# A hybrid decoder layer on one core: the first 512 tokens' q projection, by token tile or by block of input features

## The chip, the core and the metric

The kernel runs on one core of a Trainium2 chip. The metric is the device time of one execution in microseconds (us), lower is better. Before the change the runs shown gave a median of 1939.51 us (three runs, 1933.7 to 1939.64).

The engines are named as in the profile: PE (TensorE; PEld is its weight load), ACT (ScalarE), DVE (VectorE), POOL (GpSimd), SP (SyncE, which here only issues DMAs). SPq and ACTq are the sequencers of SP and ACT, which issue DMAs in order.

## The reference

x has 2048 tokens of 1024 features, all in float32. The layer is

```python
h = rms_norm(x, attn_norm_g)
z = h @ w_in                     # 512 q, 128 k, 128 v, 3 x 512 conv columns
q, k = rms_norm(q), rms_norm(k)  # per head of 64
y_attn = swa_sink_attention(q, k, v, sinks)      # window 128
y_conv = gate_b * short_conv(gate_c * xc, conv_w)
x = x + concat(rms_norm(y_attn), rms_norm(y_conv)) @ w_out
hm = rms_norm(x, mlp_norm_g)
x = x + square(relu(hm @ w_up)) @ w_down
```

The part that the change touches is `z = h @ w_in` for the first 512 tokens and the first 768 columns (q, k, v).

## The kernel before, in words

**Products.** Each float32 operand is split into a high part (rounded to PE's float32r format, by ACT) and a low part (the rest, by DVE). A product is three matmuls: high by high, high by low, low by high. In the projections to z's rows the stationary operand is a 128x128 block of h (features by tokens) and the moving one 256 or 512 columns of the weights.

**Chunks.** The mixers (attention, convolution, output projection) run over four chunks of 512 tokens, each of four token tiles of 128. While the attention of chunk c goes on, `besides` (line 941) does beside it chunk c's convolution and half of its output projection, then chunk c+1's norm, transposes and q/k/v projection; `fill` with the counts of `FILL` decides how the two are interleaved, and the priorities in `PRIO` steer the scheduler. After the mixers comes the MLP, in blocks of 512 (lines 1096 to 1545), which the change leaves as it is.

**The first chunk's start** (lines 436 to 541) has its order written out by hand for all engines (`manual_schedule`). x0 are four token tiles [128 tokens, 1024 features], loaded on SP: tile 0 in two halves, then the first 256 columns of w_in in two halves of input features, then tiles 1 to 3, then the next 256 columns. PE first turns `SPIN[0]` = 5 idle matmuls, then the transposes of tile 0 (`moved(0, 0)`, line 468), then `SPIN[1]` = 3 idle ones. ACT makes h's high part with the gain of attn_norm (line 474), DVE the low part (line 476), in pieces of 128 by 128; ACT and DVE split the weights (lines 458, 459). The norm's 1/rms is not in h: it is applied where z is copied out of PSUM (`put_z`, line 493). `product0` (line 488) then does one token tile after the other for columns 0 to 255. Columns 256 to 511 and 512 to 767 (k and v) follow in `project_qkv(0, ...)` (lines 557 to 578), four token tiles each, through the general helper `mm3` (lines 266 to 268). Line 1058 then transposes the 1/rms values, and the convolution's first product (pc_c) starts.

**Buffers.** Raw weights go through two `raw` buffers of [128, 2048]; split weights through four `w` buffers of that size. Two further sets matter for the change: `wop` (four buffers of [128, 2, 512], which later hold the convolution's outputs yt and the MLP's weights) and `at` (five of that size, which hold the attention's outputs). Split weights are stored to DRAM once (`keep`, line 228) and fetched by the later chunks, so that the split is done once; for q a later chunk fetches, for each half of the input features, two parts of two column pieces (line 585). x0's tiles are at the same time the rows that the residual sum is added to (line 892).

**Queues.** SP issues nearly all loads and stores in program order: the gains (lines 1061 to 1082) behind the first loads, and among them the k/v weights (line 239).

PSUM has eight banks: three `mm`, four `at`, one `tr`.

Of the kernel before, what the change touches and what calls it, by code (L numbers as in the profile page):

```python
# [7 lines left out]
F32 = mybir.dt.float32  # L8
# [8 lines left out]
P = 128  # L17
# [62 lines left out]
SPIN = (5, 3)  # L80
# [22 lines left out]
def hymba_layer(  # L103
# [99 lines left out]
    n_pieces = [0]  # L203
# [232 lines left out]
    x0 = [row("x1", f"x0_{t}", NT) for t in range(NT)]  # L436
    z0 = [zrow(f"z0_{t}") for t in range(NT)]
    raw0, raw1 = (raw_part(f"raw_qkv{pc}") for pc in range(2))
    hl0, hl1 = (high_low(0, f"w_qkv{pc}") for pc in range(2))
# [9 lines left out]
    def load_x0(t, cut=1):  # L449
        for i in range(cut):  # L450
            r = slice(i * D // cut, (i + 1) * D // cut)
            nc.sync.dma_start(x0[t][:, r], xf[t * P : (t + 1) * P, r])

    load_w0 = lambda i: nc.sync.dma_start(*cols256(wi, 0, pieces=2)(raw0)[i])

    def split0(i, raw, hl):
        r = slice(i * 512, (i + 1) * 512)
        nc.scalar.copy(hl[0][:, r], raw[:, r])
        nc.vector.tensor_tensor(hl[1][:, r], raw[:, r], hl[0][:, r].bitcast(F32), op=ALU.subtract)

    def moved(t, part):

        for i in range(2):
            kk = i * (KD // 2)
            if not part:
                pts[t, i] = bank("at", f"pt_a0_{t}_{i}")
                for j in range(4):
                    nc.tensor.transpose(pts[t, i][:, j * P : (j + 1) * P], x0[t][:, (kk + j) * P : (kk + j + 1) * P], ident)
            else:
                p3 = pts.pop((t, i)).rearrange("p (k t) -> p k t", k=4)  # L470
                dh, dl = (d[:, kk : kk + 4, t * P : (t + 1) * P] for d in h)
                for k in range(KD // 2):
                    g = g_in[kk + k]
                    nc.scalar.activation(dh[:, k], p3[:, k], AF.Copy, scale=g)
                for k in range(KD // 2):
                    nc.vector.scalar_tensor_tensor(
                        dl[:, k], p3[:, k], g_in[kk + k], dh[:, k].bitcast(F32), op0=ALU.mult, op1=ALU.subtract
                    )

    w0 = [w.rearrange("p (k c) -> p k c", k=KD) for w in hl0]  # L480

    def product0(t, i, ks=range(KD)):

        if (i, ks[0]) == (0, 0):
            pzs[t] = bank("mm", f"pz0_0_{t}")[:, :256]
        a, b = ((0, 0), (1, 0), (0, 1))[i]
        for k in ks:
            nc.tensor.matmul(
                pzs[t], h[a][:, k, t * P : (t + 1) * P], w0[b][:, k, :], start=i + k == 0, stop=i + k == KD + 1
            )  # L490

    def put_z(t):
        nc.scalar.activation(z0[t][:, :256], pzs[t], AF.Copy, scale=rs0[:, t : t + 1])

    pts, pzs = {}, {}

    with tc.manual_schedule(engines={ET.PE, ET.Activation, ET.DVE, ET.Pool, ET.SP}):
        nc.scalar.dma_start(g_rows, attn_norm_g[0].rearrange("(k p) -> k p", p=P))
        nc.scalar.activation(warm, mhalf[:, :1], AF.Square)
        load_x0(0, cut=2)  # L500
        load_w0(0)
        load_w0(1)
        for t in range(1, NT):
            load_x0(t)
        nc.sync.dma_start(*cols256(wi, 256)(raw1)[0])
# [11 lines left out]
        moved(0, 0)  # L517
        moved(0, 1)
        spin(SPIN[1])
        for i in range(4):  # L520
            split0(i, raw0, hl0)
            product0(0, 0, range(2 * i, 2 * i + 2))
            if i == 1:
                moved(1, 0)
        product0(0, 1)
        product0(0, 2)
        for t in range(1, NT):
            moved(t, 1)
            for i in range(4 if t + 1 == NT else 0):
                split0(i, raw1, hl1)  # L530
            norm_stats(x0[t - 1], f"a0_{t - 1}", rs0[:, t - 1 : t])
            if t > 1:
                put_z(t - 2)
            if t + 1 < NT:
                moved(t + 1, 0)
            for i in range(3):
                product0(t, i)
        norm_stats(x0[NT - 1], f"a0_{NT - 1}", rs0[:, NT - 1 : NT])
        put_z(NT - 2)
        put_z(NT - 1)  # L540
        rs0_in = nc.gpsimd.tensor_tensor(rs0_2, rs0, rs0, op=ALU.mult).ins


    with tc.tile_pool(name="mix_small", bufs=1) as mix_small, tc.tile_pool(name="mix", bufs=1) as mix:
# [10 lines left out]
        def project_qkv(c, h, z):  # L555

            z += z0 if not c else [zrow(f"z{c}_{t}") for t in range(NT)]
            if not c:
                keep(hl0, "qkv0")
            if not c:  # L560
                keep(hl1, "qkv1")
                for pc in range(1, 3):
                    hl = weights(cols256(wi, pc * 256), c, f"qkv{pc}") if pc > 1 else hl1
                    w4 = [w.rearrange("p (k c) -> p k c", k=KD) for w in hl]
                    for t in range(NT):
                        ps = bank("mm", f"pz{c}_{pc}_{t}")[:, :256]
                        hk = lambda s, k, t=t: h[s][:, k, t * P : (t + 1) * P]
                        for k in range(KD):
                            mm3(ps, lambda s, k=k: hk(s, k), lambda s, k=k: w4[s][:, k, :], k == 0, k == KD - 1)
                            if k % 2 and k < KD - 1:  # L570
                                yield
                        z_in.append(
                            nc.scalar.activation(
                                z[t][:, pc * 256 : (pc + 1) * 256], ps, AF.Copy, scale=rs0[:, t : t + 1]
                            ).ins
                        )
                        yield
                return

            both = []  # L580
            for half in range(2):
                hl = high_low(c, f"w_q{half}_{c}")
                for i in range(2):
                    for pc in range(2):
                        nc.sync.dma_start(
                            hl[i].bitcast(F32).rearrange("p (k c) -> p k c", k=KD // 2)[:, :, pc * 256 : (pc + 1) * 256],
                            parts_dram[f"qkv{pc}"][i].rearrange("p (k c) -> p k c", k=KD)[
                                :, half * (KD // 2) : (half + 1) * (KD // 2)
                            ],
                        )  # L590
                both.append([w.rearrange("p (k c) -> p k c", k=KD // 2) for w in hl])
# [982 lines left out]
```

## Time and profile before

| | before |
|---|---|
| median of the runs shown | 1939.51 us (1933.7 to 1939.64) |
| the profiled execution | 1936.33 us |
| its span, first to last instruction | 1934.6 us |
| PE busy | 1916.7 us |
| DVE, ACT, POOL busy | 1206.7, 837.7, 273.3 us |
| matmuls recorded | 9025 |
| data moved by DMA | 412.25 MB, mean 213 GB/s |

A line of the timeline gives start and duration in us, the engine, the line of the kernel, the operation, what it writes and reads by the program's names with the shapes, and how many were merged (x8); in brackets the idle time of the engine ahead of it and what ended that. A line of a group has the summed busy time and the mean in ns behind the bar, then the idle time of the engine just before, with the releasers. A line of the windows view has the stretch, its length, then busy time and count for PE, PEld, DVE, ACT and POOL, the clock that was granted to PE (1.00 is full), the share of the DMA engines' time and the GB/s moved. A line of the waits has who waited, for whom, the us in total, the number of times and the longest.

### The profile page before, as it was taken

How to read it: one execution, taken by the hardware profiler on the slowest of the kernel's cores; microseconds unless marked ns; L12 is line 12 of the kernel's file. 1: busy time of each engine (PE TensorE's matmuls, PEld its weight loads, DVE VectorE, ACT ScalarE, POOL GpSimd, SP SyncE). 2: the span in 40 equal slices, each digit the busy share in tenths (PEclk: the TensorE clock that was granted, in tenths of full speed). 3: DMA queues.
4: the chain of work that ended last, by engine and by line, in shares of the span. 5: the costliest groups of instructions: out<-in, count | busy, mean ns of one | idle time of the engine just before them, and what ended most of it. 6: DMA issues, size and time to landing. Idle time of an engine off the chain costs nothing.

```text
span 1934.6 us, 24806 instructions
## 1 busy us (share of the span) xinstructions
PE 1916.7 (99%) x9025; PEld 1596.0 (82%) x9025; DVE 1206.7 (62%) x1872; ACT 837.7 (43%) x1593; POOL 273.3 (14%) x473
## 2 busy tenths in 40 slices
PE   9999999999999999999999999999999999999999
PEld 9888888888888788888877888888888888888887
DVE  4885667447556768899878766666534334448541
ACT  6563445345344437445465554554422333232220
POOL 1112203312221112222201111101000000100000
PEclk9999999999999999999999999999999999999999
DMA  9774855464474787877665544437964457776631
GB/s 324 274 261 150 288 223 188 169 255 155 163 276 170 241 299 277 250 216 249 227 222 191 180 162 143 164 123 295 376 218 151 143 163 229 262 229 219 211 135 55
DMA packets 240634, 412.25 MB, mean 213 GB/s; under 512 B 51704, under 2 KB 147968, under 8 KB 228736
## 3 DMA queue, kind: packets, MB, share of 16 engines
q1 hardware_dynamic: 211824, 335.15, 51.3%
q0 software_dynamic: 15424, 51.40, 6.8%
q10 hardware_dynamic: 13264, 24.13, 3.3%
q8 instruction: 71, 1.16, 0.2%
q14 instruction: 51, 0.42, 0.1%
HBM read 284.78 MB, written 125.83 MB: 212 GB/s over the span
## 4 chain that ended last, share of the span: by engine, by line
PE 84%; issue 5%; DVE 4%; DMA 4%; ACT 2%; POOL 1%; SPq 1%; ACTq 0%; POOLq 0%; DVEq 0%
PE d L1534 31%; PE u L1427 23%; PE pout L266 2%; PE pout L268 2%; PE pout L267 2%; PE pz L266 2%; PE pz L267 2%; PE pz L268 2%; PE pc_c L266 2%; PE px_c L266 2%; PE px_c L267 2%; PE px_c L268 2%; PE pc_c L268 2%; PE pc_c L267 2%; PE psc_b L665 1%
## 5 line engine op out<-in xcount | busy, mean ns | idle before, releaser
L1427 PE MATMUL u<-op_x,wop 128*128 128x512 f32 x2688 | 612.5, 390 | 3.0 <-DVE wop L417 1.3
L1534 PE MATMUL d<-op_w,op_f 128*128 128x512 f32 x2688 | 609.4, 389 | 0.0
L1427 PEld LDWEIGHTS u<-op_x,wop 128*128 128x128 f32 x2688 | 503.7, 188 | 111.4 <-DVE wop L417 4.0
L1534 PEld LDWEIGHTS d<-op_w,op_f 128*128 128x128 f32 x2688 | 504.7, 188 | 104.6
L398 DVE TENSOR_TENSOR op_f<-op_f 128x1024 fp32r<-128x1024 f32 x112 | 136.9, 1225 | 237.8 <-ACT op_f L397 237.4
L397 ACT CAST op_f<-op_f 128x1024 fp32r<-128x1024 f32 x112 | 118.0, 1054 | 355.9 <-DMA op_f<-fop 343.7
L416 ACT CAST wop<-wu 128x512 fp32r<-128x512 f32 x156 | 96.4, 621 | 92.0 <-PE u L1427 87.7
L417 DVE TENSOR_TENSOR wop<-wu,wop 128x512 fp32r<-128x512 f32 x156 | 111.7, 717 | 34.1 <-ACT wop L416 19.0
L1163 POOL DMA_DIRECT2D fop<-s x96 | 52.3, 545 | 433.3 <-DVE s L1166 426.4
L1169 DVE TENSOR_TENSOR u<-u,u 128x512 f32<-128x512 f32 x128 | 87.8, 686 | 18.8 <-PE u L1427 18.8
L398 DVE TENSOR_TENSOR op_w<-raw,op_w 128x1024 fp32r<-128x1024 f32 x56 | 68.4, 1222 | 25.4 <-ACT op_w L397 25.4
L397 ACT CAST op_w<-raw 128x1024 fp32r<-128x1024 f32 x56 | 58.9, 1053 | 42.3 <-PE d L1534 20.1
L1175 ACT ACTIVATE u<-u 128x512 f32<-128x512 f32 x64 | 40.6, 634 | 51.7 <-DVE u L1169 50.0
L682 ACT ACTIVATE sc_b<-sc_b,ngm_b 128x128 f32<-128x128 f32 x128 | 49.9, 392 | 26.5 <-DVE ngm_b L679 26.5
L714 POOL TENSOR_SCALAR_AFFINE_SELECT pp_b<-pp_b 128x512 fp32r<-128x512 f32 x60 | 41.1, 697 | 116.9 <-ACT pp_b L707 63.4
L1376 POOL DMA_DIRECT2D wds<-raw x16 | 8.6, 535 | 333.8 <-DVE raw L1374 333.8
L416 ACT CAST wop<-wu_s 128x512 fp32r<-128x512 f32 x64 | 39.5, 621 | 35.6 <-PE u L1427 27.4
L266 PE MATMUL pout<-w_wo,yt_c 128*128 128x512 f32 x128 | 52.4, 410 | 0.0
L268 PE MATMUL pout<-w_wo,yt_c 128*128 128x512 f32 x128 | 51.9, 406 | 0.0
L267 PE MATMUL pout<-w_wo,yt_c 128*128 128x512 f32 x128 | 51.2, 400 | 0.0
L266 PE MATMUL pout<-w_wo,at_b 128*128 128x512 f32 x128 | 50.2, 395 | 0.2 <-DVE x L892 0.2
L267 PE MATMUL pout<-w_wo,at_b 128*128 128x512 f32 x128 | 50.0, 391 | 0.3 <-DVE w_wo L249 0.3
(255 smaller groups left out, 3132.7 us busy)
## 6 DMA issues: line engine op xcount, KB each, us to landing
op_f<-fop SPq DMA_DIRECT2D x112, 512.0 KB, 4.5
raw<-in_w_down_dram SPq DMA_DIRECT2D x72, 512.0 KB, 4.4
wu<-in_w_up_dram SPq DMA_DIRECT2D x128, 256.0 KB, 3.8
w_wo<-wo SPq DMA_DIRECT2D x24, 1024.0 KB, 6.8
fop<-s POOLq DMA_DIRECT2D x96, 256.0 KB, 2.7
fop<-u ACTq DMA_DIRECT2D x64, 256.0 KB, 2.3
op_x<-xop SPq DMA_DIRECT2D x28, 512.0 KB, 6.5
w_q<-qkv SPq DMA_DIRECT2D x24, 512.0 KB, 6.0
```

The source lines that it names most:

```text
L266: nc.tensor.matmul(ps, st(0), mv(0), start=first, stop=False)
L267: nc.tensor.matmul(ps, st(0), mv(1), start=False, stop=False)
L268: nc.tensor.matmul(ps, st(1), mv(0), start=False, stop=last)
L397: nc.scalar.copy(op[:, 0], raw)
L398: nc.vector.tensor_tensor(op[:, 1], raw, op[:, 0].bitcast(F32), op=ALU.subtract)
L416: splits.append(nc.scalar.copy(hi, blk).ins)
L417: nc.vector.tensor_tensor(lo, blk, hi.bitcast(F32), op=ALU.subtract)
L682: nc.scalar.activation(sc[:, hd, :], sc[:, hd, :], AF.Exp, bias=ngm[:, hd : hd + 1], accum_out=den[:, hd : hd + 1])
L1163: eng.dma_start(fop_dram[tb][ORDER_DOWN.index(i)][n // 2][:, n % 2], b)
L1169: return nc.vector.tensor_tensor(dst, ps, b, op=ALU.add).ins
L1427: nc.tensor.matmul(pt, wops[i][:, a, k, :], xops[tb, p][k // 2][:, b, k % 2, :], start=p not in GOES_ON and k + j == 0, stop=k + j == NB + ...
L1534: nc.tensor.matmul(ps[tb][j], fs[tb][:, a, k, j * P : (j + 1) * P], w[:, b, k, :], start=first and p not in GOES_ON and k + n == 0, stop=l ...
```

## The change

For the first 512 tokens the q projection (columns 0 to 511) no longer goes token tile by token tile in two column pieces. It goes by blocks k of 128 input features: for each block the weights [128, 512] are split, the block's transposes for all four token tiles fill one PSUM bank, and twelve matmuls of 512 columns add the block to four PSUM banks, one a token tile (`mm` three times and `tr`). The transposes run two blocks ahead. x0 is now one tile [128, 4, 1024], loaded by feature blocks (blocks 0 and 1 alone, then pairs), in a pool of its own that is given back after the stage; the mixers' small tiles take its place. So the residual's rows are loaded again for chunk 0 as for the others, behind the first projection.

Block 0's weights are loaded on ACT's queue. The eight split blocks lie in the four `wop` buffers and four of the `at` buffers, and are stored from there in eight transfers; later chunks fetch each half's part in one transfer. The k and v columns (512 to 767) keep their form, still with `mm3`, but stand inside the hand-written order, with their load issued when block 3 has been split. The gains' loads move ahead (q, k, sinks) or to that same place (the rest). The second idle spin goes (3 to 0). The norm's sums of squares run from block 4 on.

```diff
-SPIN = (5, 3)
+SPIN = (5, 0)
...
-    n_pieces = [0]
+    n_pieces = [2]
...
+    raw0 = [raw_part(f"raw_q{half}") for half in range(2)]
+    hl0 = [wop_pool.tile([P, 2, AW], F32R, tag="wop", name=f"w_q0_{k}", bufs=NWOP) for k in range(NWOP)]
+    hl0 += [pool.tile([P, 2, AW], F32R, tag="at", name=f"w_q0_{k}", bufs=NAT) for k in range(NWOP, KD)]
...
+        def load_x0(k, n):
+            r = slice(k * P, (k + n) * P)
+            nc.sync.dma_start(x0[:, :, r], xf[:CH, r].rearrange("(t p) c -> p t c", p=P))
...
+        def split0(k):
+            raw = by_k(raw0[k // KH])[:, k % KH]
+            nc.scalar.copy(hl0[k][:, 0], raw)
+            nc.vector.tensor_tensor(hl0[k][:, 1], raw, hl0[k][:, 0].bitcast(F32), op=ALU.subtract)
+
+        def turn(k):
+            pts[k] = bank("at", f"pt_a0_{k}")
+            for t in range(NT):
+                nc.tensor.transpose(pts[k][:, t * P : (t + 1) * P], x0[:, t, k * P : (k + 1) * P], ident)
...
+        def product0(k, order):
+            for i, t in order:
+                a, b = ((0, 0), (0, 1), (1, 0))[i]
+                nc.tensor.matmul(
+                    pzs[t],
+                    h[a][:, k, t * P : (t + 1) * P],
+                    hl0[k][:, b],
+                    start=k + i == 0,
+                    stop=k + i == KD + 1,
+                )
...
+        load_w0(nc.scalar, 0, 1)
...
+        load_x0(0, 1)
+        load_x0(1, 1)
+        load_w0(nc.sync, 1, 1)
+        for k in range(2, KD, 2):
+            load_x0(k, 2)
+            load_w0(nc.sync, k, 2)
+        load_gains(0)
...
+        turn(0)
         spin(SPIN[1])
+        turn(1)
+        pzs = [bank(tag, f"pz0_0_{t}") for t, tag in enumerate(("mm", "mm", "mm", "tr"))]
+        for k in range(KD):
+            split0(k)
+            moved(k)
+            if k == KH - 1:
+                raw = raw_part("raw_qkv2")
+                nc.sync.dma_start(*cols256(wi, AW)(raw)[0])
+                load_gains(1)
+            if k >= KH:
+                norm_stats(x0[:, k - KH], f"a0_{k - KH}", rs0[:, k - KH : k - KH + 1])
+            if k + 1 < KD:
+                product0(k, [(i, t) for i in range(3) for t in range(NT)])
+            else:
+                product0(k, [(i, t) for t in range(NT) for i in range(3)])
+            if k + 2 < KD:
+                turn(k + 2)
...
+    for half in range(2):
+        d = dram.tile([2, P, 2048], F32, name=f"q{half}")
+        parts_dram[f"q{half}"] = [d[i] for i in range(2)]
+        with tc.high_priority(offset=-LATER):
+            for k in range(KH):
+                nc.sync.dma_start(
+                    d[:, :, k * AW : (k + 1) * AW].rearrange("i p c -> p i c"), hl0[half * KH + k].bitcast(F32)
+                )
...
-            for t in range(NT if c else 0):
+            for t in range(NT):
                 r = (c * NT + t) * P
                 xr = row("x1", f"x1_{c}_{t}", NT)
-                nc.sync.dma_start(xr, xf[r : r + P, :])
+                with nullcontext() if c else tc.issue_after(z_in[-1]):
+                    nc.sync.dma_start(xr, xf[r : r + P, :])
```

In the new kernel the transposes are line 496, the wide products line 508, the weight splits lines 490 and 491, h's parts lines 500 and 501, and the transposes of 1/rms line 1070.

More of the change, by code (lines that the diff above doesn't have):

```diff
@@ L447, in hymba_layer @@
     g_in = [g_in_all[:, k : k + 1] for k in range(KD)]
[L449 to L478, printed above, removed]
@@ L555, in project_qkv @@
         def project_qkv(c, h, z):
[L557 to L591, printed above, removed]
+            z += [zrow(f"z{c}_{t}") for t in range(NT)]
+            both = [[by_k(w) for w in weights(None, c, f"q{half}")] for half in range(2)]
             w4 = [w.rearrange("p (k c) -> p k c", k=KD) for w in weights(None, c, "qkv2")]
```

122 lines of the change are left out of this document (56 added, 66 removed).

## The prediction

> **What bounds the kernel now.** I read the page's busy line and chain first, then the start of the program: the chain in order of time, the TensorE (PE) timeline and short windows.
>
> ```profile
> PE 1916.7 (99%) x9025; PEld 1596.0 (82%) x9025; DVE 1206.7 (62%) x1872; ACT 837.7 (43%) x1593; POOL 273.3 (14%) x473
> PE 84%; issue 5%; DVE 4%; DMA 4%; ACT 2%; POOL 1%; SPq 1%; ACTq 0%; POOLq 0%; DVEq 0%
> ```
>
> PE is busy for 99% of the span and is most of the chain, so a change counts when PE gets through the same products sooner. The one long piece of the chain at the start that is not PE is a load:
>
> ```profile
> 2.74 7.76 DMA x<-in_x_dram
> ```
>
> The second token tile was issued at 2.74 us and PE restarted on it at about 10.5. This is the opening on PE (start, duration, line, what; in brackets the idle time before it):
>
> ```profile
> 4.22 1.97 PE L468 MATMUL pt_a<-ident,x 128*128 128x128 f32 x8
> 8.57 1.02 PE L488 MATMUL pz<-w_qkv,h_a 128*128 128x256 f32 x4 [1.10 <-ACT w_qkv L458]
> 10.55 1.39 PE L468 MATMUL pt_a<-ident,x 128*128 128x128 f32 x8 [0.96 <-DMA x<-in_x_dram]
> 11.59 3.96 PE L488 MATMUL pz<-w_qkv,h_a 128*128 128x256 f32 x20
> 15.39 1.03 PE L468 MATMUL pt_a<-ident,x 128*128 128x128 f32 x8
> 16.18 3.12 PE L488 MATMUL pz<-w_qkv,h_a 128*128 128x256 f32 x24
> 19.14 1.04 PE L468 MATMUL pt_a<-ident,x 128*128 128x128 f32 x8
> 19.93 5.99 PE L488 MATMUL pz<-w_qkv,h_a 128*128 128x256 f32 x48
> 25.76 0.28 PE L266 MATMUL pz<-w_qkv,h_a 128*128 128x256 f32 x1
> 48.80 0.60 PE L1058 MATMUL pr<-ident,rs_row 128*128 128x128 f32 x4
> 49.15 0.48 PE L266 MATMUL pc_c<-h_a,w_wc 128*128 128x512 f32 x1
> 49.47 0.39 PE L267 MATMUL pc_c<-h_a,w_wc 128*128 128x512 f32 x1
> 49.70 0.39 PE L268 MATMUL pc_c<-h_a,w_wc 128*128 128x512 f32 x1
> ```
>
> The first projection product starts at 8.57, and all 768 columns of the four tiles are done at 48.80, where the transposes of line 1058 begin. I take that moment as the mark: before, 48.80; what is it after? Part of the loss is the clock:
>
> ```profile
> 11.00:12.00 1.00, 1.00 (x8) 1.00 (x7) 0.20 (x1) 0.76 (x3) 0.00 (x0) 0.60 1.04 383
> 12.00:13.00 1.00, 1.00 (x6) 1.00 (x6) 0.58 (x3) 1.00 (x5) 0.00 (x0) 0.50 1.07 388
> 13.00:14.00 1.00, 1.00 (x7) 1.00 (x6) 1.00 (x6) 1.00 (x3) 0.00 (x0) 0.50 1.15 316
> 14.00:15.00 1.00, 1.00 (x8) 1.00 (x7) 0.59 (x3) 0.46 (x2) 0.36 (x2) 0.69 0.65 94
> 15.00:16.00 1.00, 1.00 (x11) 1.00 (x10) 0.00 (x0) 0.00 (x0) 0.43 (x1) 1.00 0.47 39
> ```
>
> The third column from the end is the granted clock: half speed from about 11.2 to 14.6 us. The column says 1.00 at 4 us too, but eight transposes took 1.97 us at 4.22 and 1.03 at 15.39, so the start was also at half speed.
>
> **The change part by part.** *Products.* Row for the wide matmul, from the page:
>
> ```profile
> L1427 PE MATMUL u<-op_x,wop 128*128 128x512 f32 x2688 | 612.5, 390 | 3.0 <-DVE wop L417 1.3
> ```
>
> 612.5/2688 = 0.228 us for one of 512 columns. The 192 of 256 columns from 25.76 to 48.80 give 0.120. Before: 288 x 0.120 = 34.6. After: 96 x 0.228 + 96 x 0.120 = 21.9 + 11.5 = 33.4. The wide form itself is worth only 1.2 us.
>
> *Transposes.* Still 32, now in eight groups of four. Eight hold PE for 0.79 (15.39 to 16.18), a group for 0.40; the first wide matmul after transposes takes 0.32 (49.15 to 49.47) instead of 0.23. So 0.49 a group; two groups stand ahead of the first product, six between the products: 2.9.
>
> *The start.* The order of the queues in the changed program is fixed by hand: SP loads feature block 0 of x, block 1 of x, block 1 of w, then pairs; ACT's queue loads block 0 of w; PE does the transposes of blocks 0 and 1 and then the first product. So the product waits for both x blocks: with w block 0 that is 0.79 MB, with w block 1, which interleaves, 1.05 MB. What the DMAs moved at that time:
>
> ```profile
> 1.50:3.00 1.50, 1.42 (x6) 1.42 (x7) 0.00 (x0) 1.41 (x2) 0.94 (x11) 1.00 0.69 220
> 3.00:4.00 1.00, 1.00 (x6) 0.79 (x4) 0.00 (x0) 0.00 (x0) 0.00 (x0) 1.00 0.80 228
> 4.00:5.00 1.00, 1.00 (x6) 0.96 (x6) 0.17 (x1) 0.00 (x0) 0.00 (x0) 1.00 0.77 244
> 5.00:6.00 1.00, 1.00 (x7) 1.00 (x6) 0.00 (x0) 0.63 (x3) 0.00 (x0) 1.00 0.87 262
> ```
>
> Summing the last column, 0.80 MB are there at 5.0 us and 1.06 at 6.0. I take 5.5 for x block 1, plus 1.0 for its four transposes at half speed (1.97/2): first product at 6.5. Ends: 6.0 (x at 5.0), and 8.6, before's own first product, if the pieces of 512 bytes a row, which no row here shows, cost all of the lead; nearest are the rates above, so I keep 6.5. Splits and gains keep up, by these rows:
>
> ```profile
> L458 ACT CAST w_qkv<-raw_qkv 128x512 fp32r<-128x512 f32 x8 | 4.5, 645 | 0.6 <-DMA raw_qkv<-in_w_in_dram 0.6
> L459 DVE TENSOR_TENSOR w_qkv<-raw_qkv,w_qkv 128x512 fp32r<-128x512 f32 x8 | 5.1, 687 | 0.0
> L275 ACT ACTIVATE junk_a<-x 128x1024 bf16<-128x1024 f32 x4 | 4.4, 1106 | 0.0
> 14.21 0.25 ACT L275 ACTIVATION_READ_ACCUMULATOR junk_a<-x 128x1 f32 x1
> L1059 ACT COPY rs_row<-pr 128x512 f32<-128x512 f32 x1 | 0.6, 578 | 0.0
> ```
>
> Per block ACT has a cast (0.65), a scaled copy out of PSUM (near the 0.58 of line 1059) and from block 4 on a norm (1.1 + 0.25): 2.6 us. DVE has two of 0.69. PE's block is 12 x 0.228 + 0.49 = 3.2 us. If ACT were the limit of blocks 4 to 7 by the 0.6 that separates it from PE, it would have to slow by a quarter. The loads keep up too: 4.2 MB at the 240 to 410 GB/s of the rows above are there by about 16 us, when PE is at block 3.
>
> *The clock.* The second idle spin (three matmuls) goes. Before, continuous work restarted at 10.55 and the clock was full at 14.6, 4.1 us later. After, work is continuous from 5.5, so full at 9.6; the product's 3.1 us until then count half: loss 1.5. Ends: 0 (full at once), and 3.0, if half speed lasts the 6 us that passed from the first product (8.57) to 14.6. By the Trainium skill ("TensorE: Matmul & The Clock Gate", Part 1: The HAM clock gate) the clock rises only after a free-running window of about 3.4 us was busy, and falls after an idle one; taken from 5.5 that would be a loss of 1.2 to 2.9 in place of 1.5, an estimate from that page, and a gain of 3.1 to 4.8 in all. This trace agrees with a window of that length (11.2 to 14.6).
>
> *Sum.* 6.5 + 33.4 + 2.9 + 1.5 = 44.3 against 48.80: **4.5 us earlier**.
>
> *What is moved or added elsewhere.* From 8.0 (6.5 with the clock's loss) PE takes 3.2 a block. The k/v weights (1 MB) lie in the buffer of blocks 0 to 3 and are issued only when block 3 is split, near 16 us; even at 230 GB/s they land by 22, and PE wants them at 32.8: hidden by 10 us. Behind that load SP queues the conv and norm gains, four of the eight stores of split weights and the first conv weights; these wait for block 7's split (about 27) anyhow, land before 34 and are wanted at 44, and their casts on ACT stand ahead of the first k/v evacuation, which cannot come before 35.7. Zeroing of the value tiles on POOL now waits for the last reader of x; behind it stands the last tile's rsqrt, whose input is ready no sooner. The residual rows are loaded a second time, 2 MB, on SP ahead of the last conv weights of the pair:
>
> ```profile
> 65.00:70.00 5.00, 5.00 (x31) 4.39 (x31) 5.00 (x14) 1.50 (x4) 0.46 (x1) 1.00 1.01 416
> L246 DVE TENSOR_TENSOR w_wb<-raw_wb,w_wb x4: 681/683/685, 98.7 to 101.1; 128x512 fp32r<-128x512 f32 x4
> 111.18 0.39 PE L266 MATMUL pb_c<-h_a,w_wb 128*128 128x512 f32 x1
> ```
>
> 2.1 MB at 416 GB/s are 5.0 us of delay at most; those weights are split at 101.8 and used at 111.18, 9.4 us of cover. Without that cover each us of delay would be a us of PE. The later chunks fetch the q weights in two transfers a half instead of four, of the same bytes: zero, as PE waited for none. For all this I take 0, ends -1 and +2 (the waits of the hand-over below, gone or doubled in two chunks).
>
> The profiled execution took 1936.33 (span 1934.6 and 1.7 around it), so it would become 1931.8. The median of the runs shown, 1939.51, stands 3.2 above it; less 4.5 it gives the forecast, **1935.0**.
>
> **Rivals.** *Early and warm:* the x blocks land at 5.0 and the clock is full at the first product. Then 6.0 + 33.4 + 2.9 = 42.3, 6.5 us gained: 1933.0. For it: less is asked of the DMAs before the first product (0.79 MB; before, a token tile and a half of the weights, 1.05 MB, stood ahead of 8.57). Against: the rates of the first 6 us.
>
> *Supply:* blocks arrive at PE's pace or slower, PE idles between them and the clock falls back as it did at 11.2. Were the 4.2 MB to come at the 230 GB/s of the first rows, they would last to 20 us, still ahead of PE; it needs rates under 150. At that rate the last pair lands near 30, two blocks and the k/v columns follow (6.4 + 11.5), the mark is near 48, the time 1938.7. Against: the 383 to 412 rows.
>
> *Hand-over (slower):* from the second chunk on, the changed order puts the eight transposes of the probabilities (ptp_b) straight behind the scores, some 6 us earlier, and their splits on ACT and DVE with them, ahead of the evacuations of pout. This stage of before:
>
> ```profile
> PE pt_a L294 <- DVE ms_b L776: 0.6, 1, 0.6
> PE pt_a L294 <- DVE h_h L299: 0.5, 2, 0.2
> 319.44 0.41 ACT L682 ACTIVATE sc_b<-sc_b,ngm_b 128x128 f32<-128x128 f32 x1 [2.46 <-DVE ngm_b L679]
> 322.65 1.05 ACT L707 CAST pp_b<-ptp_b 128x512 fp32r<-128x512 f32 x2
> 324.36 1.28 DVE L708 TENSOR_TENSOR pp_b<-ptp_b,pp_b 128x512 fp32r<-128x512 f32 x2
> ```
>
> PE waited 1.1 there. If the casts hold ACT (1.05) and the subtractions DVE (2 x 0.64) while PE stands for a bank, and the eight exponentials (3.2 us from 319.44) fall into the same wait, a hand-over costs up to 5.5; there are two: 11 less 4.5, that is 6.5 slower, 1946. It decides from the point where both together cost over 4.5. Against: these transposes read scores made long before.
>
> That the change doesn't do what it says is out: PE's order in the stage is written out, and its 96 wide products are in the program.
>
> **How the numbers follow.** Forecast 0.66, early and warm 0.18, supply 0.08, hand-over 0.08. The runs shown lie 1933.7 to 1939.64 apart, so about 3 us of either sign ride on any difference. 0.3% (5.8 us) is about what a measurement of this kernel can tell from no change. Faster by more than that: all of early and warm and, by the scatter, 0.2 of the forecast: 0.38. Slower by more: most of hand-over, 0.07. Within: 0.55. The range for 8 in 10: from 1935.0 less the 2.0 of early and warm and the scatter, 1929.5, to the supply case, 1939.0.
>
> **What would show it.** Right: the first product (wide, line 508) between 6 and 7.5 us, twelve of them in 2.7 us once the clock is full, no PE idle time inside the eight blocks, line 1070's transposes near 44.3, no new PE wait for a DMA. Wrong: PE idle ahead of a pt_a or pz of the stage with a DMA as releaser; granted clock 0.5 past 11 us; a PE wait of over 2 us near 300 or 470; wb weights split later than PE wants them.

## The result, and the profile after

The changed kernel took 1941.68 us (median of 16 executions, 1939.03 to 1944.62) against 1936.71 us for the kernel before on the same chip (16 executions, 1931.94 to 1941.29). The ratio is 1.0024, 95% interval [1.0017, 1.0031]: about 4.6 us slower, where 4.5 us faster was forecast. Ratios here leave out disturbed executions, so they are not exactly the quotient of the medians.

The two lines of the page that answer to the first ones of the prediction, from the profiled execution after (1943.26 us, span 1941.6):

```profile
PE 1917.8 (99%) x8923; PEld 1589.3 (82%) x8923; DVE 1202.1 (62%) x1848; ACT 831.5 (43%) x1565; POOL 271.7 (14%) x473
PE 80%; DVE 6%; issue 5%; DMA 4%; ACT 2%; POOL 2%; SPq 0%; ACTq 0%; POOLq 0%; DVEq 0%
```

PE is as busy as before to 1.1 us. Its share of the chain fell from 84 to 80%, and what grew is the waiting on DVE (4 to 6%). So the products did not get dearer: PE waits somewhere. It is not in the stage that was changed. PE's timeline of that stage after, with its columns as before:

```profile
5.64 0.66 PE L496 MATMUL pt_a<-ident,x 128*128 128x128 f32 x4 [0.49 <-DMA x<-in_x_dram]
6.70 2.81 PE L508 MATMUL pz<-w_q,h_a 128*128 128x512 f32 x11 [0.41 <-ACT h_a L500]
...
25.66 0.60 PE L496 MATMUL pt_a<-ident,x 128*128 128x128 f32 x4
26.01 5.74 PE L508 MATMUL pz<-w_q,h_a 128*128 128x512 f32 x24
31.59 0.28 PE L266 MATMUL pz<-w_qkv,h_a 128*128 128x256 f32 x1
```

The first wide product starts at 6.70 and the last has given way to the k/v columns at 31.59; nothing stands between the blocks. The clock was full from the first product on: the windows that showed 0.50 to 0.69 before (from 11 to 15 us) read

```profile
11.00:12.00 1.00, 1.00 (x6) 0.83 (x5) 1.00 (x2) 0.41 (x1) 0.00 (x0) 1.00 1.08 387
14.00:15.00 1.00, 1.00 (x6) 0.83 (x5) 0.85 (x2) 0.62 (x2) 0.00 (x0) 1.00 0.46 148
```

To see where the lead went I set the start of the same matmul in both traces against each other. "Shift" is after less before, in us, so negative is a lead. In the changed kernel it is -5.70 at the last k/v product (43 us), -3.97 at 56, -2.48 at 95, +1.53 at 112, -0.52 at 158, +1.47 at 645 and +6.86 from 750 us to the end. The losses lie in three places.

**First chunk.** PE's waits from 40 to 130 us (what waited, for what; in total, times, the longest):

```profile
PE po_b L767 <- DVE pp_b L722: 1.9, 1, 1.9
PE ptq_b L652 <- DVE z L641: 1.5, 1, 1.5
PE psc_b L679 <- DVE qt_b L658: 0.7, 1, 0.7
```

The 0.7, at 82 us, is in most of the kernels below. Behind the 1.5 (PE's wait for q's transposes, ptq_b, at 45.9 us) stands ACT, whose queue at 37 us shows the reason (the second line is the first k/v evacuation, whose product was done by 34.5):

```profile
37.28 2.18 ACT L245 CAST w_wc<-raw_wc 128x512 fp32r<-128x512 f32 x4 [4.74 <-DMA raw_wc<-in_w_in_dram]
39.37 0.47 ACT L571 ACTIVATE z<-pz,rs 128x256 f32<-128x256 f32 x1
```

The casts of the first conv weights (raw_wc) stand in the program's order ahead of the evacuation, and the load came only at 37.3. Behind the 1.9 stands DVE, here after and then before, and after that PE:

```profile
103.71 1.90 DVE L246 TENSOR_TENSOR w_wb<-raw_wb,w_wb 128x512 fp32r<-128x512 f32 x3 [6.03 <-DMA wc<-w_wc]
105.52 0.68 DVE L722 TENSOR_TENSOR pp_b<-ptp_b,pp_b 128x512 fp32r<-128x512 f32 x1
```

```profile
98.70 1.89 DVE L246 TENSOR_TENSOR w_wb<-raw_wb,w_wb 128x512 fp32r<-128x512 f32 x3
100.51 0.69 DVE L708 TENSOR_TENSOR pp_b<-ptp_b,pp_b 128x512 fp32r<-128x512 f32 x1
```

```profile
103.00:107.00 4.00, 2.12 (x9) 1.25 (x8) 3.29 (x6) 1.55 (x4) 0.00 (x0) 1.00 0.70 293
107.00:111.00 4.00, 4.00 (x15) 3.23 (x14) 3.79 (x7) 2.12 (x5) 0.19 (x1) 0.57 0.79 188
```

The probabilities' lower halves (pp_b) stand on DVE behind the split of the wb weights, and that split now waits 6.03 us for a store of wc, which frees its buffer; before it waited for none. PE was busy for 2.12 of the 4 us to 107, and in the next 4 us the granted clock was 0.57.

**Hand-overs.** The two rows of waits that the prediction watched (295 to 335 us, then 466 to 506 us):

```profile
PE pt_a L294 <- DVE h_h L299: 1.2, 2, 0.9
```

```profile
PE pt_a L294 <- DVE h_h L299: 1.4, 3, 0.9
```

Before they were 0.5 (shown with the prediction) and, from 466 to 506 us,

```profile
PE pt_a L294 <- DVE h_h L299: 0.7, 2, 0.5
```

The shift grows by 1.09 and 1.17 us there. No wait of over 2 us, the sign that the prediction named, stands in these stretches.

**The MLP's start**, 700 to 740 us. PE's waits, and SP's timeline of the same stretch, first after, then before:

```profile
PE u L1421 <- ACT wop L416: 3.1, 2, 2.9
PE pout L266 <- DMA w_wo<-wo: 1.3, 1, 1.3
```

```profile
696.98 0.80 SPq L396 DMA_DIRECT2D op_x<-xop  x2
716.29 0.38 SPq L411 DMA_DIRECT2D wu<-in_w_up_dram  x1
716.77 1.03 SPq L396 DMA_DIRECT2D op_x<-xop  x2
717.85 2.17 SPq L411 DMA_DIRECT2D wu<-in_w_up_dram  x3
```

```profile
695.32 0.80 SPq L396 DMA_DIRECT2D op_x<-xop  x2
696.17 0.42 SPq L411 DMA_DIRECT2D wu<-in_w_up_dram  x1
696.68 13.99 SPq L396 DMA_DIRECT2D op_x<-xop  x2
710.73 10.04 SPq L411 DMA_DIRECT2D wu<-in_w_up_dram  x8
```

The issues have the same order, but the first fetch of an MLP weight (wu) goes out at 716.29 in place of 696.17, and the other weights behind it 7 us later (717.85 for 710.73). SP's own waits name what held it:

```profile
SPq L411 <- PE pout L268: 13.7, 1, 13.7
```

A weight fetch can wait for an output product only through its buffer. The table of buffers of the built programs says which: tiles of the MLP's pool lie where the mixers' pool was, and the places in that pool are given out in the order in which its kinds of buffer are first asked for. The change asks for `at` early and for the residual rows last, and the places moved: the first wu tile lay on rows of z before and lies on the `raw` buffer that holds a part of the last `w_wo` now, which the last output products (pout) read. After PE's wait of 2.86 us at 726.83 the clock is halved again (0.57 from 728 to 732).

### The profile page after: what moved, and what is told of

Read it like the earlier page. It is cut to its first block, busy times and chain, and to the rows that moved or that the text cites. A ratio compares the mean times of both kernels' runs of the same rounds, so it can differ in the third digit from the quotient of the medians.

```text
span 1941.6 us, 24543 instructions
## 1 busy us (share of the span) xinstructions
PE 1917.8 (99%) x8923; PEld 1589.3 (82%) x8923; DVE 1202.1 (62%) x1848; ACT 831.5 (43%) x1565; POOL 271.7 (14%) x473
## 4 chain that ended last, share of the span: by engine, by line
PE 80%; DVE 6%; issue 5%; DMA 4%; ACT 2%; POOL 2%; SPq 0%; ACTq 0%; POOLq 0%; DVEq 0%
PE d L1528 31%; PE u L1421 24%; PE pout L266 2%; PE pout L268 2%; PE pout L267 2%; PE pz L266 2%; PE pz L267 2%; PE pz L268 2%; PE px_c L268 1%; PE px_c L266 1%; PE px_c L267 1%; PE po_b L767 1%; PE pc_c L266 1%; PE pc_c L268 1%; PE pc_c L267 1%
```

## The experiments

Three theories. **Places** (L in the expectations): the MLP's start is late because buffers moved in SBUF, the cores' on-chip memory. **Traffic** (T): the first chunk loses its lead to 2 MB that are loaded a second time and to the stores of the split weights, both ahead of conv weights on SP. **Order** (H): fetching the q weights in two transfers a half changed the planned order at the hand-overs. The rival to all is that the lead is lost whatever is done, because transfers set the first chunk's end.

The shifts against the profile of the kernel before, at five matmuls (last k/v product, end of the first chunk's convolution, the last out products of the second chunk and of the fourth's first half, and the last product of all), with the ratio of the timed runs, each against the kernel before on the same chip (interval about +-0.0009, or 1.8 us), and what it makes of 1937 us:

| run | 43 | 125 | 297 | 645 | end | ratio | us |
|---|---|---|---|---|---|---|---|
| changed | -5.70 | +1.53 | -0.51 | +1.47 | +6.86 | 1.0024 | +4.6 |
| e10 changed again | -4.29 | -2.34 | -2.93 | -1.23 | +2.50 | 1.0027 | +5.2 |
| e1 places of before | -5.53 | -2.82 | -3.25 | -1.30 | -0.62 | 1.0006 | +1.2 |
| e2 before, new places | +0.75 | +0.75 | -0.35 | -0.23 | +5.80 | 1.0015 | +2.9 |
| e3 four fetches | -5.92 | -0.51 | -0.66 | -0.03 | +3.51 | 1.0007 | +1.4 |
| e4 stores later | -5.84 | +0.12 | -0.60 | +1.42 | +4.69 | 1.0033 | +6.4 |
| e5 no second load | -3.59 | -1.66 | -3.81 | -1.99 | +3.47 | 1.0007 | +1.4 |
| e6 k/v before casts | -3.98 | -1.95 | -4.08 | -2.17 | +3.28 | 1.0017 | +3.3 |
| e7 rows resident, e1, e3 | -4.48 | -2.20 | -4.13 | -3.81 | -3.36 | 0.9988 | -2.3 |
| e8 e7 with stores later | -3.90 | -3.17 | -0.05 | +1.23 | +4.39 | 1.0004 | +0.8 |
| e9 e1 and e3 | -4.58 | +0.20 | +0.30 | +0.72 | -0.08 | 1.0004 | +0.8 |
| e11 e8, x rows early | -3.66 | -3.72 | -4.93 | -5.01 | -2.44 | 0.9983 | -3.3 |
| e12 e7 and e6 | -4.19 | -1.62 | -2.78 | -2.26 | -1.48 | 0.9997 | -0.6 |

A row is one profile, against one profile of the kernel before. Another profile of that same first stage (e2) stands at +0.75 at 43 us, with 6.83 us at half clock where the first had 3.41; so a lead here is known to about 1 us. The columns between 43 and 645 tell the losses apart: 43 to 297 is the first chunk and what its end gives back, 297 to 645 the hand-overs, 645 to the end the MLP's start.

### e1_layout and e2_before_places: only the places

```diff
+    x_held = [row("x1", f"x_held{t}", NT) for t in range(NT)]
     z0 = [zrow(f"z0_{t}") for t in range(NT)]
     raw0 = [raw_part(f"raw_q{half}") for half in range(2)]
-    hl0 = [wop_pool.tile([P, 2, AW], F32R, tag="wop", name=f"w_q0_{k}", bufs=NWOP) for k in range(NWOP)]
-    hl0 += [pool.tile([P, 2, AW], F32R, tag="at", name=f"w_q0_{k}", bufs=NAT) for k in range(NWOP, KD)]
     h = parts(pool, "h", "a0")
...
     g_rows = pool.tile([P, CHP], F32, tag="s2", name="g_rows", bufs=4)[:KD, :P]
+    xt_first = [row("xt", f"xt_first{i}", 2) for i in range(2)]
+    hl0 = [wop_pool.tile([P, 2, AW], F32R, tag="wop", name=f"w_q0_{k}", bufs=NWOP) for k in range(NWOP)]
+    hl0 += [pool.tile([P, 2, AW], F32R, tag="at", name=f"w_q0_{k}", bufs=NAT) for k in range(NWOP, KD)]
```

> The changed kernel with one edit: the buffers of the work pool are handed out in the order of the kernel before (residual rows, z, raw, the two halves of h, s2, xt, output buffers), by four residual rows that are allocated first and left unused and by allocating the output buffers after xt. Every engine's instructions stand in the same order as in the changed kernel; only the places in SBUF differ. Theory L (places): in the changed kernel the first weight fetches of the MLP lie on buffers that the last output projection still reads, so that the fetch that was issued at 696.2 us before is issued at 716.3 us; that is where the shift of the matmuls against the kernel before grows from +1.47 us (at 646 us) to +6.86 us (at 750 us). L expects this growth to go, the fetch to be issued near 697 us, and the time to fall by 4 to 6 us against the changed kernel, to about the kernel before (within 1 us). Theory T (traffic: the second load of the residual rows and the stores of the split weights make the conv weights late) and theory H (the hand-over's order in the second and third chunk) expect no change from this edit: 4.9 us above the kernel before.

> The kernel before with one edit: its work pool handed out in the changed kernel's order (residual rows last, output buffers ahead of h). No instruction moves on any engine. Theory L expects the same 4 to 6 us to appear here, at 700 to 740 us of the profile and nowhere else: 1941 to 1943 against 1936.7. Theories T and H expect the time of the kernel before within 0.5 us. If it comes out between, L has only a part of the loss at the start of the MLP.

e1: ratio 1.0006 [0.9997, 1.0015], so 3.5 us of the 4.6 are gone (4 to 6 were expected); in the profile the MLP's start costs +0.68 in place of +5.39. e2, the kernel before with nothing but the other order of first requests: 1.0015 [1.0006, 1.0025], 2.9 us where 4 to 6 were expected, and +6.03 in the profile between 645 and 750 us. SP's timeline in e1, then in e2:

```profile
695.21 0.42 SPq L411 DMA_DIRECT2D wu<-in_w_up_dram  x1
695.73 17.13 SPq L396 DMA_DIRECT2D op_x<-xop  x2
```

```profile
712.90 0.38 SPq L411 DMA_DIRECT2D wu<-in_w_up_dram  x1
713.38 1.03 SPq L396 DMA_DIRECT2D op_x<-xop  x2
```

The fetch moves from 716 to 695 in the one and from 696 to 713 in the other, with no instruction moved in either. Places are shown as a cause, from both sides. The size by time, 2.9 to 3.5 us, is less than the 5.4 to 6.0 of these profiles and no more than what the second load makes by time (below). The seven profiles with the changed places lose 3.3 to 6.0 us here, and of six with the old ones (new stage) four lose -0.8 to +0.8, but e8 3.2 and e11 2.6. In e11 a wait of 2.04 us for split MLP weights at 732.85 met a halved clock as well. In e8 the halved clock stands elsewhere, from 675.3 to 678.7 behind a wait of 1.71 us at 674.1 (PE's pa_b, released by ACT's xm); at the MLP's start it waits 2.4 us at full clock. So with the old places too PE can wait about 2 us there.

### e3_four_fetches: the hand-overs

```diff
-            both = [[by_k(w) for w in weights(None, c, f"q{half}")] for half in range(2)]
+            for half in range(2):
+                hl = high_low(c, f"w_q{half}{c}")
+                for i in range(2):
+                    for pc in range(2):
+                        cs = slice(pc * 256, (pc + 1) * 256)
+                        nc.sync.dma_start(by_k(hl[i].bitcast(F32))[:, :, cs], by_k(parts_dram[f"q{half}"][i])[:, :, cs])
```

> The changed kernel with one edit: in chunks 1 to 3 each half of the q weights is fetched in four transfers of 256 columns, as before, and not in two. From the second chunk on every engine's instructions then stand in the order of the kernel before. Theory H: the two fewer instructions per half moved the score transposes of the third block up at both hand-overs (313 and 485 us), which cost 1.09 us (shift -0.52 to +0.57) and 1.17 us (+0.31 to +1.48) there. H expects both steps to go and the time to fall by about 2.2 us against the changed kernel. L and T expect no change; the shift at 150 us stays near -0.5 and the growth at the MLP's start stays.

The ratio is 1.0007 [0.9998, 1.0017]. In the profile the steps at the hand-overs are +0.59 and +0.01 (1.09 and 1.17 without the edit), so only the second is gone. PE's waits of the two stretches say the same; they were 1.2 and 1.4:

```profile
PE pt_a L294 <- DVE h_h L299: 1.1, 2, 0.9
```

```profile
PE pt_a L294 <- DVE h_h L299: 0.7, 2, 0.5
```

Over all profiles 297 to 645 us costs 1.7 to 2.0 us in the six with two transfers (the changed kernel twice, e1, e4, e5, e6) and -0.1 to +0.6 in five of the six with four (1.3 in e8). That the fetches' form costs time is shown, about 1.4 us of it at the hand-overs; the time fell by 3.3 us, within its interval of that and of the 2.2 expected. That it acts through the order and not through the transfers is read from the waits, which are for DVE and not for a DMA. This profile also shows what the first chunk can lose: PE waited 2.96 us for ptq_b at 47.13, where the changed kernel's first profile had 1.54, with half clock from 46.6 to 50.0.

### e4_stores_later: the stores behind the first conv load

```diff
-        with tc.high_priority(offset=-LATER):
+    def keep_q(last):
+        with tc.high_priority(offset=-LATER), tc.issue_after(last):
...
+            got = nc.sync.dma_start(dst, src)
+        if name == "wc0":
+            keep_q(got.ins)
```

> The changed kernel with one edit: the eight stores of the split q weights are queued on SyncE behind the load of the first conv weight tile (raw_wc), where six of them stood ahead of it; the residual rows and the next chunk's first two row loads are held behind the load of the second pair's wx tile, where they stood, so that they don't take the place of the stores. Theory T, its first part: the stores made raw_wc land at 37.25 us (33.1 before), so that its casts on ScalarE held up the first k/v evacuation and the q transposes waited 1.54 us at 45.9 us. Expected: raw_wc lands by 33, that wait goes, the shift at 56 us is -5.5 (it was -3.97); 1.5 us of the time comes back if nothing later takes it, less if the wait at 106 us (1.88 us, and then 3.41 us at half clock) takes it. A rival within T, that the wait at 45.9 us is made by the order on ScalarE and not by the landing, expects the same wait of 1.0 to 1.5 us even with raw_wc at 33. L and H expect no change at the MLP's start and the hand-overs from this.

Besides the stores, the edit holds the residual rows and two rows of the next chunk behind the second pair's wx load. The load of raw_wc lands at 31.9, the evacuation starts at 34.52, and the wait at 45.9 us is gone; the shift stays -5.84 up to 107 us:

```profile
32.30 2.17 ACT L250 CAST w_wc<-raw_wc 128x512 fp32r<-128x512 f32 x4
34.52 0.48 ACT L577 ACTIVATE z<-pz,rs 128x256 f32<-128x256 f32 x1
```

Then it is lost at once, further on. PE's waits from 100 to 130 us, with the clock at half from 111.5 to 114.9:

```profile
PE pb_c L273 <- DVE w_wb L251: 3.3, 2, 2.3
```

The ratio is 1.0033 [1.0022, 1.0044], no better than the changed kernel. So the stores make raw_wc late, as T says, but moving them moves the lateness to the second pair's weights: no gain in time. I had kept open "less if the wait at 106 us takes it", not a loss of all.

### e5_no_reload: without the second load

```diff
-                with nullcontext() if c else tc.issue_after(z_in[-1]):
-                    nc.sync.dma_start(xr, xf[r : r + P, :])
+                if c:
+                    nc.sync.dma_start(xr, xf[r : r + P, :])
+                else:
+                    nc.gpsimd.memset(xr, 0.0)
```

> The changed kernel without the four loads that fetch the first chunk's residual rows a second time (2 MB on SyncE at 72 to 75 us): the rows are filled with zeros on GpSimd at about 2 us, so the first chunk's residual is left out of the result. SyncE's next loads move up by four places; no other engine's order changes. Theory T, its second part: these 2 MB hold up the second pair's raw_wb (issued 87.69, landed 97.2) and the stores behind it that free the split buffers, so that ScalarE and VectorE, which work in order, reach the first block's probabilities late, and the matmuls wait 1.88 us at 106.35 us and run at half clock for 3.41 us. Expected: raw_wb lands by 93, no wait over 0.6 us between 95 and 112 us, no half clock there, the shift at 125 us is between -3.5 and -2.5 (it was +1.53), and the time falls by 1.5 to 3 us (part of the 4.0 us came back by 158 us anyway). The rival: the second wait is only what the first one (1.54 us at 45.9 us, raw_wc late) passes on, and the reload is innocent: then the wait at 106 us stays within 0.5 us of 1.9. Hand-overs and the MLP's start (+1.1, +1.2, +5.4 us) are expected unchanged by both.

The ratio is 1.0007 [0.9999, 1.0016], 3.3 us better than the changed kernel. No wait over 0.7 us is left between 40 and 130 us. But raw_wb lands at 95.2, not by 93, so the mechanism was not quite the one I wrote. The trace shows it on SP: the load of raw_wb is issued at 86 to 89 us in every kernel whose stores stand as they did, when its buffer is free. Without the second load the first of the two stores of wc goes out ahead of it, at 81.45 (79.42 in the kernel before); with it both are queued behind, at 88.1 and 88.7. They land at 101.2 and 103.6, and the wb split waits for them. SP's timeline after, then before:

```profile
87.69 0.38 SPq L239 DMA_DIRECT2D raw_wb<-in_w_in_dram  x1
88.12 1.27 SPq L228 DMA_DIRECT2D wc<-w_wc  x2
```

```profile
79.42 0.33 SPq L228 DMA_DIRECT2D wc<-w_wc  x1
86.47 0.38 SPq L239 DMA_DIRECT2D raw_wb<-in_w_in_dram  x1
86.90 0.57 SPq L228 DMA_DIRECT2D wc<-w_wc  x1
```

No run moves that store alone, so the share of its place and that of the 2 MB are not told apart. In the five other kernels that keep the transfers as changed (e1, e3, e6, e9, e10) that split starts on DVE between 99.9 and 104.0, in e5 and e7 at 98.8 and 97.9. At 106 us PE waited 0.5 to 1.9 us where it was 103.2 or later (the changed kernel, e3, e9), and less than 0.4 where it was 101.3 or earlier (e1, e6, e10). e9 and e7, of which e7 has no second load (it also keeps the rows of a chunk in one tile and zeroes the value tiles in another order on POOL):

```profile
103.95 1.90 DVE L246 TENSOR_TENSOR w_wb<-raw_wb,w_wb 128x512 fp32r<-128x512 f32 x3 [6.36 <-DMA wc<-w_wc]
105.76 0.68 DVE L731 TENSOR_TENSOR pp_b<-ptp_b,pp_b 128x512 fp32r<-128x512 f32 x1
```

```profile
97.91 1.89 DVE L246 TENSOR_TENSOR w_wb<-raw_wb,w_wb 128x512 fp32r<-128x512 f32 x3
99.71 0.69 DVE L728 TENSOR_TENSOR pp_b<-ptp_b,pp_b 128x512 fp32r<-128x512 f32 x1
```

### e6_kv_before_casts: the order on ScalarE

```diff
-        with ahead(7):
+        with ahead(7), tc.issue_after(z_in[0]) if name == "wc0" else nullcontext():
```

> The changed kernel with one edit: the casts and differences of the first conv weight tile are queued on ScalarE behind the first k/v evacuation, where they stood ahead of it. The transfers stay as they are (raw_wc is expected to land near 37 us again). The theory that the order on ScalarE made the wait at 45.9 us: the first k/v block is evacuated at 34.5 to 35 us and not at 39.37, the q transposes find their rows, and the shift at 56 us is below -5 (it was -3.97). The rival: VectorE has the differences of raw_wc in order ahead of the q/k scaling too, or the conv products themselves wait for the late tile, so 1 us or more of the wait stays, at 43 to 47 us. For the time both expect little, 0 to 1.5 us less than the changed kernel, since the later losses are untouched.

A miss: the evacuation moved ahead of the casts, to 36.38 in a profile whose lead was 1.7 us smaller, but PE now waits 1.7 us for the k transposes at 49.4, and the shift at 56 us is -1.88 from -3.98. The ratio is 1.0017 [1.0006, 1.0027]. That wait ends with DVE's z, so the late load is passed on along DVE just as well; the order on ACT alone is not the cause.

### e7 to e9 and e12: together

> The changed kernel with three edits that leave its first stage as it is: the first 512 rows of x go straight into the residual buffers (one tile of four rows per chunk) and stay there, so the second load is gone; the work pool is handed out in the order of the kernel before; the q weights are fetched in four transfers per half as before. If the losses are the three that the theories name and add up, the shift is -5.5 at 43 us, about -3.5 at 125 and 158 us (the 1.5 us at 45.9 us and 0.7 us at 82 us stay, since the stores still stand ahead of raw_wc), about -3 after the two hand-overs and between -2.5 and -3.5 at the end: 1933.5 to 1934.5 against 1936.7 to 1937.2. If the gain of the first stage is lost wherever it goes (the rest of the program being set by transfers), the shift goes back to about 0 by 160 us in this kernel too, and the time is that of the kernel before.

e7 makes x0 the tile of the first chunk's residual rows and drops the second load:

```diff
-        x0 = first.tile([P, NT, D], F32, name="x0")
+    x0 = pool.tile([P, NT, D], F32, tag="x1", name="x0", bufs=1)
...
+            xs = pool.tile([P, NT, D], F32, tag="x1", name=f"x1_{c}", bufs=1) if c else x0
             for t in range(NT):
                 r = (c * NT + t) * P
-                xr = row("x1", f"x1_{c}_{t}", NT)
-                with nullcontext() if c else tc.issue_after(z_in[-1]):
-                    nc.sync.dma_start(xr, xf[r : r + P, :])
-                x1.append(xr)
+                if c:
+                    nc.sync.dma_start(xs[:, t], xf[r : r + P, :])
+                x1.append(xs[:, t])
```

It took 1934.37 us against 1937.09 before, ratio 0.9988 [0.9980, 0.9997]: faster than both, with 3.4 us of the stage's lead of 4.5 still there at the end. So the lead is not lost whatever is done; the rival is out.

> The kernel of e7 with the edit of e4 as well: seven of the eight stores of the split q weights stand behind the first conv pair's loads, and none ahead of raw_wc. Without the second load of the rows there is room for these stores between 40 and 70 us. Expected if traffic alone is late: the shift stays near -5.8 to 100 us, as in e4, and the waits for w_wb that e4 showed at 107 and 112 us (0.97 and 2.33 us) are gone or below 0.7 us in all, so that the time is 1931.5 to 1932.5. If the stores between 45 and 75 us delay the second pair's weights by themselves, the waits for w_wb at 105 to 112 us stay above 2 us and the shift at 158 us is above -2.5, no better than e7.

e8 was expected best and is not: 1.0004 [0.9995, 1.0013]. Up to 112 us it loses nothing (-3.96), then PE waits at the transposes of the next chunk's rows, whose loads I had held back on SP to 85 us, and the clock is at half from 125.8 to 129.2:

```profile
124.45 0.66 PE L299 MATMUL pt_a<-ident,xt_a 128*128 128x128 f32 x4 [2.53 <-DVE ms_b L809]
```

> The changed kernel with the edits of e1 (places) and e3 (four fetches) and the second load of the rows kept: e7 without its resident rows. If the parts add up (e1 -3.7 us against the changed kernel from its own run, e3 -2.1, e7 -7.3), this is 1935.5 to 1936.5 against 1937 for the kernel before, and what is left to e7's 1934.4 is the second load, 1.0 to 2.5 us. If the second load costs nothing once places and order are right, it equals e7 within 0.5 us.

e9 is 1.0004 [0.9995, 1.0013]: against e7 the second load is worth 3.1 us by time and 3.3 at the end of the profiles, more than the 1.0 to 2.5 expected, though the interval of a difference of two ratios (2.5 us) holds both.

> The kernel of e7 with the edit of e6 (the casts of the first conv tile behind the first k/v evacuation). In e6 this moved the evacuation but the k transposes then waited 1.67 us at 49.4 us, so that by 56 us 2.1 us were lost, no less than without it (1.7). If the order on ScalarE costs anything of its own, e12 is 0.5 us or more below e7; expected is no difference within 0.7 us, either sign.

e12 is 0.9997 [0.9988, 1.0006], no gain over e7: in its profile the k transposes again wait 1.7 us.

### e10_changed_again, and e11_rows_stores_early_x

> The changed kernel unaltered, on the chip of these runs, for a second profile. Shown twice is a cause that the program makes: the first matmul of the MLP's weights is expected to wait 2.5 to 3.5 us near 727 us again, with half clock after it, and the steps of about 1.1 us at the two hand-overs. What the landing times make may differ: the wait of 1.88 us at 106 us with its 3.41 us at half clock was not in e1, e3 or e6, whose first chunk has the same transfers; it is expected here with a chance of a half. Time 4 to 5 us above the kernel before.

Time 1.0027 [1.0016, 1.0038] again. The wait at the MLP's start (2.74 us at 722.62, half clock from 723.1 to 726.5) and the steps at the hand-overs (1.11 and 0.85) repeat; the wait at 106 us does not, its wb split came at 101.3. The lead at 43 us is -4.29 here: the first profile's -5.70 was a good one.

> The kernel of e8 with the next chunk's first two row loads not held back: they stand ahead of raw_wc again, so that only two loads of 0.5 MB and no store go ahead of it. In e8 the transposes of these rows waited 2.53 us at 124.45 us, with 3.41 us at half clock behind. Theory T: that wait goes, raw_wc still lands by 35, the shift stays between -4.5 and -6 up to 125 us and at 158 us; with nothing at the hand-overs and the MLP's start the time is 1932 to 1933.5, below e7 by 1 to 2 us. The rival, that any 4 MB moved into the time from 45 to 75 us come back as late weights of the second pair: the time is that of e7 or above.

e11 is e8 without holding back the two x rows. It took 1932.93 us against 1935.85, ratio 0.9983 [0.9973, 0.9994], the best of all; the 3.3 us and e7's 2.3 lie within each other's intervals. raw_wc landed at 34.0, and between 40 and 130 us its trace lists no PE wait of 0.2 us or more; at 645 us the lead is 5.01. Half of it is then lost at the MLP's start, with a halved clock:

```profile
PE u L1437 <- ACT wop L419: 2.3, 2, 2.0
```

## Why the prediction was wrong

- **The stage** was right. First product: 6.5 predicted, 6.70 measured. Blocks and k/v columns: 24.9 and 11.4 us (6.70 to 31.59 to 42.96), with 24.8 and 11.5 from the prediction's rows; of the 1.5 us for the clock nothing was lost in this profile. Mark: 4.5 us earlier predicted; the lead at the last k/v product is 3.6 to 5.9 us in the twelve profiles that have the new stage, 4.64 in the mean. What differs most among them is the clock's start, the term of 1.5 (0 to 3.0): full clock is first shown between 4.8 and 11.1 us, in three profiles ahead of the first product, which starts at 6.26 to 7.55. So the warm half of "early and warm" is one of the stage's ordinary states and no rival; early (6.0) it was in none.
- **The step that failed is "everything downstream 0, ends -1 and +2"**. It cost 12.6 and 6.8 us in the two profiles of the changed kernel, 9.1 by time (4.6 + 4.5), from four causes. Three of them stand in the text with the wrong price; the fourth, the places, is not in it at all.
- *Places.* The prediction followed instructions, queues and bytes, but not where buffers lie. 2.9 to 3.5 us by time.
- *The second load.* "5.0 us of delay at most ... 9.4 us of cover" took the cover up to PE's own use of the wb weights. But their split stands in order on ACT and DVE ahead of pp_b, which PE wanted at 104.5 (106.35 less the wait), some 4 us before those weights (111.18 less the lead of 2.48). The bytes were also not all of the delay: a store that frees a buffer changed its place in SP's queue. About 3 us by time.
- *The conv weights,* "land before 34": 37.25, behind six stores of 0.5 MB. Two were issued at 10.7; the four from 25.1 on the prediction had counted and given no time. The wait that this made was 1.5 us at 45.9 in the first profile and 0.2 to 3.0 in the others with the same order up to there; e4 and e11, without these stores ahead, have none.
- *Two fetches for four,* "zero, as PE waited for none". The DMAs were indeed not waited for; the order that went with them cost about 1.4 us. The hand-over rival had named that order (ptp_b some 6 us earlier), at a chance of 0.08 and up to 11 us; of that the size failed.
- **Not settled:** how often the first chunk loses its lead in the changed kernel (5.2 us in one profile, 1.4 in the other, up to 297 us), and why e6, which keeps the second load, lost nothing from 43 to 297 us. The parts by time (3.5, 3.3 and 3.3 for e1, e3 and e5 alone) sum to 10 us, while e7, which has all three, gains 7.0; with intervals of 1.8 us each I can't say whether they overlap.

## What to carry to other kernels

When a change asks for buffers in another order, compare the table of places before and after as one compares the order of instructions: a pool that follows may wait for other readers, far from the change. The cover of a transfer ends at the first thing that stands behind its consumer in an engine's order, not at the consumer's own deadline. And a lead that was won is only kept if the loads, stores and rows of the next stages come earlier too; here the same new stage gave +4.6 us with the second load, the new places and the new fetches, and -2.3 to -3.3 us without them.

## What the runs showed of the hardware that was not expected

- A wait much shorter than the half-clock span behind it can be followed by half clock: 1.88 us at 106.35 us was followed by 3.41 us at half. But e9's wait of 1.90 us at the same place, and e2's of 3.13 us at 723.7, were not. By the Trainium skill ("TensorE: Matmul & The Clock Gate", Part 1: The HAM clock gate) the clock is judged in free-running windows of about 3.4 us and falls after an idle one. The halved stretches here, 3.41 us or twice that, agree with the length; that a wait of 1.88 us was enough does not agree with an idle window. That the wait's place in such a window parts the cases is not shown.
- The moment of full clock moves the start: it was first shown at 4.82 us in the changed kernel's profile and at 11.06 in e5's, and the wide products of the first stage take 399 and 423 ns in the mean, with the same program on PE, ACT and DVE in that stage:

```profile
L508 PE MATMUL pz<-w_q,h_a 128*128 128x512 f32 x96 | 23.9, 399 | 0.4 <-ACT h_a L500 0.4
```

```profile
L508 PE MATMUL pz<-w_q,h_a 128*128 128x512 f32 x96 | 25.8, 423 | 0.3 <-ACT h_a L500 0.3
```
